# A hybrid encoder layer on one core: sums of weights made by adding transfers in DRAM, and three of eight pairs of k-tiles as seven products

## The chip, the core and the metric

The kernel runs on one core of one Trainium2 chip. Its engines work side by side, each through its own queue in order: TensorE (PE in the profile) multiplies into PSUM, ScalarE (ACT), VectorE (DVE) and GpSimd (POOL) do the elementwise work, SyncE (SP) issues nearly all transfers. Each waits on semaphores of the others. The metric is the device time of one execution in microseconds (us).

## The reference

One layer over 256 tokens of width 2048, all in float32:

```
hn   = rmsnorm(x) ;  proj = hn @ w_in          # 2048 x 18432, nine blocks of 2048 columns
q, v, f_fwd, f_bwd, z_a, b_gate, c_gate, h_b, z_b = split(proj)
o_a  = head_rmsnorm(hgrn2(silu(q), v, f_fwd) + reversed hgrn2(.., f_bwd)) * silu(z_a)   # group A, 16 heads
o_b  = rmsnorm(b_gate * conv3(c_gate * h_b)) * silu(z_b)                                # group B
h    = x + concat(o_a, o_b) @ w_out            # 4096 x 2048
h    = h + (p @ w_ple) * sigmoid(h @ w_ple_gate)
out  = rmsnorm(h)
```

## The kernel before, in words

**Precision.** Every operand of a large product is split into a high part (a cast to fp32r) and a low part (what the cast left). A product is then three matmuls: high by high, high by low, low by high (`three`, L799). ScalarE makes the high part of the weights (L107), VectorE the low one (L108).

**The stream of weights.** `Stream` (L28 to L118) loads weights in order into three raw buffers of a megabyte (`load`, L79, issued by SyncE), and splits them in parts of 1024 columns into five `spl` buffers. `get` (L110) splits three parts ahead of the one that PE is about to use, with priority over other work. A raw buffer is free for the next load when its last part has been split.

**Order of the work.** The kernel is written in the order of PE's matmuls; a scheduler then sets the order on each engine's queue from priorities, and what stands in a queue waits for what is ahead of it. Each k-tile of the large products calls `tick` (L278), which counts and starts work that was put off by `at` (L275). In groups A and B a tick is about 0.7 us of PE.

- Group A: four rounds of two pairs of heads (`two_pairs`, L624). For each pair e = 0, 1 of a round PE makes the two forget gates and q (48 ticks), whose results are moved out of PSUM (`evac`, L378) into `xf` and `qt`; then v and z for both pairs (64 ticks). `mix_forgets` (L428) multiplies `xf` by the tokens' norms on POOL (`by_norms`, L388), and ScalarE takes its sigmoid (L432) and logarithm; `mix_pair` (L485) makes the decays and the products' operands, among them `qc`, `kc` (L529) and `kx` (L535) on POOL. In rounds 2 to 4 the `xf` of pair 1 stands on POOL right behind pair 0's `kx`.
- Group B: eight rounds of four products of 16 ticks (`cg`, `hb`, twice more `hb`), with the convolution on VectorE and POOL.
- The output projection: columns in two steps u of two blocks of 512, each with a half for group A's results (`mixa`) and one for group B's (`mixb`). A half (L805) has 16 k-tiles, taken as eight pairs q. A pair has two k-tiles, two blocks of tokens and two of columns, so eight block products of three matmuls, 24. For q = 3 and 5 (`SUMS`, L171) it is done in seven products, 21 matmuls, from sums of the four weight blocks and of the activations' blocks. The main accumulators take four PSUM banks, the seven-product pairs four more (`extra`); behind the last of these pairs VectorE puts the four extra banks together (L889 to L900: `d`, `v`, `d7`, `v7`), and at the half's end adds the main banks into `hh` (`add_h`, L869).
- The gate, the input embedding and the last norm end the kernel.

**Where the sums are made.** Weights: `sums` (L60) adds blocks on VectorE inside the raw buffer (L66), three additions a pair, between that pair's splits; one raw buffer gives seven blocks in four parts. Activations: `act_sums` (L687) makes and splits `suma` in rounds 4 and 5 of group B and `sumb` at the start of the projection.

Of the kernel before, what the change touches and what calls it, by code (L numbers as in the profile page):

```python
# [17 lines left out]
P = 128  # L18
# [9 lines left out]
class Stream:  # L28
# [19 lines left out]
        self.where += [(j, h) for h in range(k * n // 1024)]  # L48
        return list(range(first, len(self.where)))

    def add_sums(self, *srcs):


        j = len(self.todo)
        self.todo.append((srcs, 2, 1024))
        first = len(self.where)
        self.where += [(j, h) for h in ("singles", "single", "pairs", "more")]
        return list(range(first, len(self.where)))

    def sums(self, j, h):  # L60

        b = self.raws[j].rearrange("p (b n) -> p b n", b=4)

        def add(out, in0, in1):
            with self.tc.high_priority(offset=300):
                self.nc.vector.tensor_tensor(out=out, in0=in0, in1=in1, op=ALU.add)  # L66

        if h == "singles":
            return b[:, 0:2]
        if h == "single":  # L70
            return b[:, 3:4]
        if h == "pairs":
            add(out=b[:, 0:3:2], in0=b[:, 0:3:2], in1=b[:, 2:4])
            return b[:, 0:3:2]
        add(out=b[:, 3], in0=b[:, 0], in1=b[:, 3])
        add(out=b[:, 1], in0=b[:, 3], in1=b[:, 1])
        return b[:, 1:4:2]

    def load(self, j, k0=0, k1=None, pool=None):  # L79
        srcs, k, n = self.todo[j]  # L80
        if j not in self.raws:
            tag = f"raw{j}" if pool else "raw"
            self.raws[j] = (pool or self.rawp).tile([P, 2048], F32, tag=tag, name=f"raw{j}")
        dst = self.raws[j][:, : k * n].rearrange("p (b k n) -> p b k n", b=len(srcs), k=k)
        for b, src in enumerate(srcs):
            self.nc.sync.dma_start(dst[:, b, k0:k1], src[:, k0:k1])

    def open(self, i):
        j, h = self.where[i]
        srcs, k, n = self.todo[j]  # L90
        if j not in self.raws:
            self.load(j)
        part = self.home[i] if i in self.home else self.splp.tile([P, 2048], F32R, tag="spl", name=f"spl{i}")
        if isinstance(h, str):
            r = self.sums(j, h)
            nb = r.shape[1]
            self.parts[i] = part[:, : nb * 1024].rearrange("p (b s n) -> p b s n", b=nb, s=2)
            return r, self.parts[i]
        self.parts[i] = part.rearrange("p (k s n) -> p k s n", s=2, n=n)
        kp, nb = 1024 // n, len(srcs)  # L100
        half = self.raws[j][:, : k * n].rearrange("p (b k n) -> p k b n", b=nb, k=k)[:, kp * h : kp * h + kp]
        if nb == 1:
            return half[:, :, 0, :], self.parts[i]
        return half, part.rearrange("p (k s b n) -> p k s b n", s=2, b=nb, n=n // nb)
# [17 lines left out]
def tile_hymba_encoder(  # L122
# [45 lines left out]
        for c in (B_CG, B_HB, B_BG, B_ZB):  # L168
            blocks[c, i] = sum((ws.add(w_in[c + i, h]) for h in range(2)), [])

    SUMS = (3, 5)  # L171
    oblocks = []
    for u in range(2):
        srcs = [[w_out[2 * u + n, q // 2, :, 2 * (q % 2) : 2 * (q % 2) + 2] for n in range(2)] for q in range(16)]
        oblocks.append([(ws.add_sums if q % 8 in SUMS else ws.add)(*srcs[q]) for q in range(16)])
    gblocks, pblocks = [], []
    for j in range(4):
        if j:
# [96 lines left out]
    def at(dt, fn):  # L275
        pend.append((now[0] + dt, len(pend), fn))

    def tick():  # L278
        now[0] += 1
        due = sorted(e for e in pend if e[0] <= now[0])  # L280
        for e in due:
            pend.remove(e)
        for e in due:
            e[2]()
# [399 lines left out]
    last_two[0]()  # L684


    def act_sums(src, dst, a, s):  # L687


        dve.tensor_tensor(out=a, in0=src[:, :, 0], in1=src[:, :, 1], op=ALU.add)  # L690
        a11, a21, a12, a22 = (a[:, k, m * P : (m + 1) * P] for k in range(2) for m in range(2))
        for o, x, y in ((0, a21, a22), (1, a21, a11), (2, a11, s[:, 0]), (3, a12, s[:, 2])):
            dve.tensor_tensor(out=s[:, o], in0=x, in1=y, op=ALU.subtract)
        act.copy(out=dst[:, :, 0], in_=s)
        dve.tensor_tensor(out=dst[:, :, 1], in0=s, in1=dst[:, :, 0], op=ALU.subtract)


    mixb = None
# [7 lines left out]
    for i in range(8):  # L706
# [31 lines left out]
        if i == 0:  # L738
            assert not pend
            actx.close()  # L740
            bp = mctx.enter_context(tc.tile_pool(name="bp", bufs=1, side="right", reuse_waits="tile"))
            mixb = bp.tile([P, NH, 2, T], F32R, name="mixb")
            og = bp.tile([P, 2, 2, 2, P], F32, name="og")
            suma = bp.tile([P, 2, 4, 2, P], F32R, name="suma")
        if i == 2:
            for e in range(2):
                act.copy(out=og[:, e], in_=kept[e])
        if i in (4, 5):
            a = bp.tile([P, 2, T], F32, tag="sa", name=f"sa{i}")
            b = bp.tile([P, 4, P], F32, tag="sb", name=f"sb{i}")  # L750
            k = 2 * SUMS[i - 4]
            act_sums(mixa[:, k : k + 2], suma[:, i - 4], a, b)
        hi, lo = mixb[:, 2 * i : 2 * i + 2, 0, :], mixb[:, 2 * i : 2 * i + 2, 1, :]
        act.copy(out=hi, in_=cg)
        dve.tensor_tensor(out=lo, in0=cg, in1=hi, op=ALU.subtract)


    def norm_b():
# [21 lines left out]

    sctx = ExitStack()
    spare = sctx.enter_context(tc.tile_pool(name="spare", bufs=1, side="left", reuse_waits="tile"))
    sumb = spare.tile([P, 2, 4, 2, P], F32R, name="sumb")
    tmp = spare.tile([P, 4, 512], F32, name="tmp")

    def gemm_tok(acc, ids, lhs, todo=((0, slice(0, 512)), (1, slice(0, 512)))):

# [17 lines left out]
    def half(main, extra, parts, src, sums):  # L805


        banks = None
        for q, ids in enumerate(parts):
            k = 2 * q  # L810
            if len(ids) == 2:
                for kk in range(2):
                    w = ws.get(ids[kk])[:, 0].rearrange("p s (b n) -> p b s n", b=2)
                    for n in range(2):
                        for m in range(2):
                            ah, al = (src[:, k + kk, s, m * P : (m + 1) * P] for s in range(2))
                            three(main[m][n], al, ah, w[:, n], k + kk == 0, k + kk == NKT - 1)
                        tick()
                continue
            if banks is None:  # L820
                banks = extra()
            z = SUMS.index(q)
            st, sp = z == 0, z == len(SUMS) - 1

            def one(kk, m):
                return [src[:, k + kk, s, m * P : (m + 1) * P] for s in (1, 0)]

            def some(o):
                return [sums[:, z, o, s] for s in (1, 0)]

            w = ws.get(ids[0])
            three(banks[0], *one(0, 0), w[:, 0], st, sp)
            three(main[0][0], *one(1, 0), w[:, 1], False, False)
            tick()
            w = ws.get(ids[1])
            three(main[0][1], *some(3), w[:, 0], False, False)
            w = ws.get(ids[2])
            three(banks[1], *some(0), w[:, 0], st, sp)
            tick()
            three(banks[2], *some(1), w[:, 1], st, sp)  # L840
            w = ws.get(ids[3])
            three(main[1][0], *one(1, 1), w[:, 0], False, False)
            tick()
            three(banks[3], *some(2), w[:, 1], st, sp)
            if sp:
                yield banks

    def h_transposed(u, z):

        for kk in range(2):  # L850
            tag = ("x", "y", "sc0", "sc1")[2 * z + kk]
            tp = psm.tile([P, 512], F32, tag=tag, name=f"ht{u}_{z}_{kk}")
            kt = 8 * u + 4 * z + 2 * kk
            for k in range(2):
# [9 lines left out]
    def four(pool_, name):  # L864
        if pool_ is psg:
            return [psg.tile([P, 512], F32, tag="g", name=f"{name}_{b}") for b in range(4)]
        return [psm.tile([P, 512], F32, tag=t, name=f"{name}_{t}") for t in ("x", "y", "sc0", "sc1")]

    def add_h(m, cs, v, scale):  # L869
        h = hh[:, m, cs]  # L870
# [5 lines left out]
    for u in range(2):  # L876
        cs = [slice(512 * (2 * u + n), 512 * (2 * u + n + 1)) for n in range(2)]
        for src, sums, main, other, scale in ((mixa, suma, psg, psm, False), (mixb, sumb, psm, psg, True)):
            name = f"p{'ab'[scale]}{u}"
            acc = four(main, name)  # L880
            parts = oblocks[u][8 * scale : 8 * scale + 8]
            if u == 0 and not scale:
                for z in range(2):
                    k = 2 * SUMS[z]
                    act_sums(
                        mixb[:, k : k + 2], sumb[:, z], tmp[:, 0:1].rearrange("p b (k t) -> p (b k) t", k=2),
                        tmp[:, 1:2].rearrange("p b (o t) -> p (b o) t", o=4),
                    )
            for q1, q5, q7, q6 in half([acc[0:2], acc[2:4]], lambda: four(other, "e" + name), parts, src, sums):  # L889
                d, v, d7, v7 = (tmp[:, b] for b in range(4))  # L890
                add_h(0, cs[0], q1, scale)
                act.copy(out=d, in_=q1)
                dve.tensor_tensor(out=d, in0=d, in1=q6, op=ALU.subtract)
# [173 lines left out]
```

## Time and profile before

| what | value |
|---|---|
| median of 3 runs | 1122.08 us (1121.8 to 1122.35) |
| the profiled execution, its own time | 1121.94 us |
| its span in the profile | 1120.2 us |
| PE busy | 1110.8 us (99%), granted clock 0.998 |
| VectorE, ScalarE, POOL busy | 788.6, 644.7, 216.5 us |
| group A, group B, projection | to 485, to 839, to about 1011 us |

In a row of the profile's groups stand line, engine, operation, what is written from what, the shapes and the count; then busy time and the mean of one in ns; then the engine's idle time just ahead of it and what ended that. In a timeline a row has the start in us, the duration in us, and in brackets the idle time before it with its releaser. A table by stretches has busy time and count of PE, weight loads, VectorE, ScalarE and POOL, then PE's clock, the share of the 16 DMA engines, and GB/s.

### The profile page before, as it was taken

To read this page: it belongs to the slowest core of one execution; us is meant where nothing else is said; L and a number is where in the kernel's file an instruction comes from. 1 tells how busy PE (TensorE), PEld (TensorE's weight loads), DVE (VectorE), ACT (ScalarE), POOL (GpSimd) and SP (SyncE) were. 2 spreads that over 40 slices of the span, in tenths; PEclk is the share of its full clock that TensorE was granted. 3 is DMA by queue.
4 is the path that set the end of the run, shared out by engine and by line. 5 is a ranking of instruction groups with operands and counts; after the bars stand their busy time and mean duration, and the time that the engine had idled before them with its cause. 6 is when DMAs were issued, how large, how long until landed. Compare 5 with 4: busy or idle time off the path is not lost.

```text
span 1120.2 us, 16504 instructions
## 1 busy us (share of the span) xinstructions
PE 1110.8 (99%) x6506; PEld 955.9 (85%) x6506; DVE 788.6 (70%) x1016; ACT 644.7 (58%) x892; POOL 216.5 (19%) x167
## 2 busy tenths in 40 slices
PE   9999999999999999999999999999999999999997
PEld 8888888888888888888888888888888888888886
DVE  7898476956876587766665566566559988886664
ACT  7796577756765586564454444444545454455553
POOL 1144025300522035211121111111211000000012
PEclk9999999999999999999999999999999999999999
DMA  9756445455545545546555555555556664656552
GB/s 346 281 166 212 154 162 189 156 188 184 196 143 194 183 154 185 189 150 223 174 205 188 188 189 188 188 188 188 189 190 223 225 225 151 225 202 225 202 169 75
DMA packets 41981, 214.27 MB, mean 191 GB/s; under 512 B 4656, under 2 KB 5040, under 8 KB 26288
## 3 DMA queue, kind: packets, MB, share of 16 engines
q1 hardware_dynamic: 41616, 212.88, 55.4%
q8 instruction: 51, 0.84, 0.3%
q10 hardware_dynamic: 288, 0.34, 0.1%
q14 instruction: 26, 0.21, 0.1%
HBM read 211.11 MB, written 2.10 MB: 190 GB/s over the span
## 4 chain that ended last, share of the span: by engine, by line
PE 99%; ACT 0%; DVE 0%; DVEq 0%; issue 0%; ACTq 0%
PE a L351 37%; PE a L349 19%; PE a L372 5%; PE a L370 5%; PE a L371 5%; PE pg L794 3%; PE pg L796 3%; PE pg L795 3%; PE pa L801 2%; PE pa L803 2%; PE pa L802 2%; PE pb_sc L801 1%; PE pb_sc L803 1%; PE pb_sc L802 1%; PE scps L548 1%; PE cx L592 1%
## 5 line engine op out<-in xcount | busy, mean ns | idle before, releaser
L108 DVE TENSOR_TENSOR spl<-raw,spl 128x1024 fp32r<-128x1024 f32 (+2 forms) x414 | 512.7, 1248 | 243.8 <-ACT spl L107 242.6
L351 PE MATMUL a<-xs,spl 128*128 128x512 f32 x1792 | 619.7, 394 | 0.0
L107 ACT CAST spl<-raw 128x1024 fp32r<-128x1024 f32 (+2 forms) x414 | 415.1, 1011 | 307.0 <-PE a L349 162.2
L349 PE MATMUL a<-xs,spl 128*128 128x256 f32 x1792 | 493.6, 278 | 0.0
L351 PEld LDWEIGHTS a<-xs,spl 128*128 128x128 f32 x1792 | 335.0, 188 | 76.1
L349 PEld LDWEIGHTS a<-xs,spl 128*128 128x128 f32 x1792 | 336.2, 188 | 1.5
L370 PE MATMUL a<-spl,xs 128*128 128x512 f32 x256 | 100.8, 394 | 0.0
L372 PE MATMUL a<-spl,xs 128*128 128x512 f32 x256 | 99.8, 390 | 0.0
L371 PE MATMUL a<-spl,xs 128*128 128x512 f32 x256 | 99.7, 389 | 0.0
L383 ACT COPY r<-a 128x256 f32<-128x256 f32 x112 | 40.8, 368 | 54.4 <-PE a L349 54.4
L944 POOL TENSOR_TENSOR hh<-hh,fw 128x512 f32<-128x512 f32 (+1 forms) x9 | 11.3, 1262 | 255.8 <-ACT gt L943 253.2
L372 PEld LDWEIGHTS a<-spl,xs 128*128 128x128 f32 x256 | 48.1, 188 | 10.1
L370 PEld LDWEIGHTS a<-spl,xs 128*128 128x128 f32 x256 | 48.1, 188 | 9.6
L371 PEld LDWEIGHTS a<-spl,xs 128*128 128x128 f32 x256 | 48.1, 188 | 9.5
L794 PE MATMUL pg<-spl,ht 128*128 128x512 f32 (+1 forms) x120 | 45.2, 377 | 0.0
L388 POOL TENSOR_TENSOR xf<-xf,rbc 128x1024 f32<-128x1024 f32 x8 | 19.8, 2479 | 130.9 <-DVE xf L384 124.0
L795 PE MATMUL pg<-spl,ht 128*128 128x512 f32 (+1 forms) x120 | 45.1, 376 | 0.0
L796 PE MATMUL pg<-spl,ht 128*128 128x512 f32 (+1 forms) x120 | 45.1, 375 | 0.0
L529 POOL TENSOR_TENSOR qc<-pf,ge 128x256 f32<-128x256 f32 x16 | 33.8, 2116 | 38.9 <-ACT ge L516 21.0
L801 PE MATMUL pa<-spl,mixa 128*128 128x512 f32 x104 | 40.7, 392 | 0.0
L802 PE MATMUL pa<-spl,mixa 128*128 128x512 f32 x104 | 40.5, 390 | 0.0
L803 PE MATMUL pa<-spl,mixa 128*128 128x512 f32 x104 | 40.5, 390 | 0.0
(263 smaller groups left out, 1270.6 us busy)
## 6 DMA issues: line engine op xcount, KB each, us to landing
raw<-in_w_in_dram SPq DMA_DIRECT2D x106, 1024.0 KB, 4.9
raw<-in_w_in_dram SPq DMA_DIRECT2D x74, 512.0 KB, 4.9
raw<-in_w_out_dram SPq DMA_DIRECT2D x64, 512.0 KB, 4.7
raw<-in_w_gate_dram SPq DMA_DIRECT2D x12, 1024.0 KB, 4.9
raw<-in_w_gate_end_dram SPq DMA_DIRECT2D x8, 512.0 KB, 4.9
xf<-in_xtok_dram SPq DMA_DIRECT2D x2, 1024.0 KB, 11.9
hh<-in_xtok_dram SPq DMA_DIRECT2D x1, 2048.0 KB, 10.1
raw<-in_w_ple_dram SPq DMA_DIRECT2D x4, 512.0 KB, 3.7
```

The lines of the kernel that those rows point to most:

```text
L107: self.nc.scalar.copy(out=v[:, :, 0], in_=r)
L108: self.nc.vector.tensor_tensor(out=v[:, :, 1], in0=r, in1=v[:, :, 0], op=ALU.subtract)
L349: pe.matmul(a[:, :T], lhsT=lhsT, rhs=xs[:, kt, 0, :], start=False, stop=(kt == NKT - 1))
L351: pe.matmul(a, lhsT=lhsT, rhs=xs[:, kt, :, :].rearrange("p s n -> p (s n)"), start=(kt == 0), stop=False)
L370: pe.matmul(acc[m], lhsT=lh, rhs=w[:, kt % 2, 0, :], start=(kt == 0), stop=False)
L371: pe.matmul(acc[m], lhsT=lh, rhs=w[:, kt % 2, 1, :], start=False, stop=False)
L372: pe.matmul(acc[m], lhsT=ll, rhs=w[:, kt % 2, 0, :], start=False, stop=(kt == NKT - 1))
L794: pe.matmul(acc[m], lhsT=lh, rhs=wh, start=(kt == 0), stop=False)
L795: pe.matmul(acc[m], lhsT=lh, rhs=wl, start=False, stop=False)
L796: pe.matmul(acc[m], lhsT=ll, rhs=wh, start=False, stop=(kt == nk - 1))
L801: pe.matmul(acc, lhsT=ah, rhs=w[:, 0], start=start, stop=False)
L802: pe.matmul(acc, lhsT=ah, rhs=w[:, 1], start=False, stop=False)
```

## The change

1. In each half three pairs, q = 2, 3 and 4, are done in seven products, and the pairs are taken in the order 0, 1, 2, 6, 3, 7, 4, 5: one plain pair follows the last seven-product pair, where two did.
2. The sums of weights are no longer made by VectorE. For each of the 12 seven-product pairs there is a tensor `sums` in DRAM. SyncE copies the pair's left and right blocks into it (`prepare`, two transfers of 512 KB), and POOL then issues three transfers that add while they write (`add_up`): 512 KB, then 256 KB, then 256 KB, each on what the one before has written. A table `plan` sets the ticks: preparation n (0 to 11) is copied at tick 150 + 78 n and added at 18, 36 and 54 ticks behind that. Group A ends at tick 640, group B at 1152.
3. In the projection such a pair now fills two raw buffers, one with three single blocks, one with the four sums.
4. Activations: `suma` is made in rounds 1 to 3 of group B (counted from 0), the float32 sums for `sumb` in rounds 2 to 4 (kept in `scm` and `tri`, which group A no longer needs) and split at the projection's start. Two of the four buffers in which the extra banks are put together are now `og`, and the extra banks are taken in another order (`FOUR`).

The core of the diff (line numbers in the profile of before are those of the listing above):

```diff
-    def add_sums(self, *srcs):
+    def add_sums(self, left, right, sums):
         j = len(self.todo)
-        self.todo.append((srcs, 2, 1024))
+        self.todo += [([(left, 0), (right[:, 1:2], 2)], 3, None), ([(sums, 0)], 4, None)]
         first = len(self.where)
-        self.where += [(j, h) for h in ("singles", "single", "pairs", "more")]
+        self.where += [(j, slice(0, 2)), (j, slice(2, 3)), (j + 1, slice(0, 3, 2)), (j + 1, slice(1, 4, 2))]
...
-    SUMS = (3, 5)
+    ORDER, SUMS = (0, 1, 2, 6, 3, 7, 4, 5), (2, 3, 4)
+    dramp = ctx.enter_context(tc.tile_pool(name="dramp", bufs=1, space=bass.MemoryType.DRAM))
...
+    def prepare(n):
+        srcs, sums = prepared[n]
+        for h in range(2):
+            tc.keep_in_program_order(nc.sync.dma_start(sums[:, 2 * h : 2 * h + 2], srcs[h]))
+
+    def add_up(n, step):
+        (_, right), sums = prepared[n]
+        dst, src = ((sums[:, 0:3:2], right), (sums[:, 3], sums[:, 0]), (sums[:, 1], sums[:, 3]))[step]
+        tc.keep_in_program_order(pool.dma_start(dst, src, accum_op=ALU.add))
+
+    plan = {}
+    for n in range(len(prepared)):
+        t = 150 + 78 * n
+        plan[t] = lambda n=n: prepare(n)
+        for step in range(3):
+            plan[t + 18 * (step + 1)] = lambda n=n, step=step: add_up(n, step)
+
     def tick():
         now[0] += 1
+        if now[0] in plan:
+            plan.pop(now[0])()
...
-        if i in (4, 5):
-            a = bp.tile([P, 2, T], F32, tag="sa", name=f"sa{i}")
-            b = bp.tile([P, 4, P], F32, tag="sb", name=f"sb{i}")
-            k = 2 * SUMS[i - 4]
-            act_sums(mixa[:, k : k + 2], suma[:, i - 4], a, b)
...
+        for src, z in ((mixa, i - 1), (mixb, i - SUMS[0])):
+            if 0 <= z < len(SUMS):
+                k = 2 * SUMS[z]
...
-        for q, ids in enumerate(parts):
+        for q, ids in zip(ORDER, parts):
...
-                d, v, d7, v7 = (tmp[:, b] for b in range(4))
+                d, v, d7, v7 = tmps
```

**POOL, in the last round of group A, before.** From pair 0's operands (`qc`, `kc`, `kx`) to pair 1's `xf` and `qt`, the queue has:

```order
L529 TENSOR_TENSOR qc_3763<-pf_3739,ge_3749 128x256
L529 TENSOR_TENSOR kc_3762<-dd_3740,ge_3749 128x256
L535 TENSOR_TENSOR kx_3768<-kc_3762,ge_3749 128x512
L388 TENSOR_TENSOR xf_3770<-xf_3770,rbc 128x1024
L388 TENSOR_TENSOR qt_3771<-qt_3771,rbc 128x512
```

Pair 1's `xf` stands directly behind `kx`.

The same place on POOL, now (`sums_1_4_86` is the tensor of preparation 5):

```order
L546 TENSOR_TENSOR qc_3802<-pf_3778,ge_3788 128x256
L546 TENSOR_TENSOR kc_3801<-dd_3779,ge_3788 128x256
L552 TENSOR_TENSOR kx_3807<-kc_3801,ge_3788 128x512
L284 DMA sums_1_4_86<-in_w_out_dram 256x1x512
L284 DMA sums_1_4_86<-sums_1_4_86 128x512
L405 TENSOR_TENSOR xf_3809<-xf_3809,rbc 128x1024
L405 TENSOR_TENSOR qt_3810<-qt_3810,rbc 128x512
```

Two adding transfers have come between `kx` and `xf`, and the second reads what the first writes. In the two rounds ahead of this one, preparations 1 and 3 put one transfer into the same place; the three of preparations 0, 2, 4 stand together behind the round's last work on POOL, ahead of the next round's first `xf`.

**VectorE, at the end of the projection's first half, before.** The extra banks (`epa`) are put together between splits, and the first main bank (`pa_0`) is added behind that:

```order
L893 TENSOR_TENSOR tmp<-tmp,epa_sc_7724 128x512
L108 TENSOR_TENSOR spl_7880<-raw_7862,spl_7880 128x1024
L894 TENSOR_TENSOR tmp<-epa_y,tmp 128x512
L895 TENSOR_TENSOR tmp<-tmp,epa_sc_7723 128x512
L108 TENSOR_TENSOR spl_7898<-raw_7895,spl_7898 128x1024
L896 TENSOR_TENSOR tmp<-tmp,epa_sc_7723 128x512
L874 TENSOR_TENSOR hh<-pa_0_7606,hh 128x512
```

There the four steps `d`, `v`, `d7`, `v7` are L893 to L896, and `pa_0` comes last.

The same place on VectorE, now:

```order
L920 TENSOR_TENSOR tmp<-tmp,epa_y 128x512
L95 TENSOR_TENSOR spl_7976<-raw_7955,spl_7976 128x1024
L95 TENSOR_TENSOR spl_7994<-raw_7991,spl_7994 128x1024
L921 TENSOR_TENSOR tmp<-epa_sc_7783,tmp 128x512
L905 TENSOR_TENSOR hh<-pa_0_7707,hh 128x512
L95 TENSOR_TENSOR spl_8017<-raw_7991,spl_8017 128x1024
L922 TENSOR_TENSOR og<-tmp,epa_x 128x512
L923 TENSOR_TENSOR og<-tmp,epa_x 128x512
```

The addition of `pa_0` and a split have moved ahead of `d7` and `v7` (L922, L923), which free the last extra bank.

More of the change, by code (lines that the diff above doesn't have):

```diff
@@ L49, in add @@
         return list(range(first, len(self.where)))
-    def add_sums(self, *srcs):
+    def add_sums(self, left, right, sums):
         j = len(self.todo)
-        self.todo.append((srcs, 2, 1024))
+        self.todo += [([(left, 0), (right[:, 1:2], 2)], 3, None), ([(sums, 0)], 4, None)]
         first = len(self.where)
-        self.where += [(j, h) for h in ("singles", "single", "pairs", "more")]
+        self.where += [(j, slice(0, 2)), (j, slice(2, 3)), (j + 1, slice(0, 3, 2)), (j + 1, slice(1, 4, 2))]
         return list(range(first, len(self.where)))
[L60 to L77, printed above, removed]
     def load(self, j, k0=0, k1=None, pool=None):
@@ L83, in load @@
             self.raws[j] = (pool or self.rawp).tile([P, 2048], F32, tag=tag, name=f"raw{j}")
+        if n is None:
+            blocks = self.raws[j].rearrange("p (b n) -> p b n", b=4)
+            for src, b0 in srcs:
+                self.nc.sync.dma_start(blocks[:, b0 : b0 + src.shape[1]], src)
+            return
         dst = self.raws[j][:, : k * n].rearrange("p (b k n) -> p b k n", b=len(srcs), k=k)
@@ L93, in open @@
         part = self.home[i] if i in self.home else self.splp.tile([P, 2048], F32R, tag="spl", name=f"spl{i}")
-        if isinstance(h, str):
-            r = self.sums(j, h)
+        if n is None:
+            r = self.raws[j].rearrange("p (b n) -> p b n", b=4)[:, h]
             nb = r.shape[1]
@@ L169, in tile_hymba_encoder @@
             blocks[c, i] = sum((ws.add(w_in[c + i, h]) for h in range(2)), [])
-    SUMS = (3, 5)
-    oblocks = []
+    ORDER, SUMS = (0, 1, 2, 6, 3, 7, 4, 5), (2, 3, 4)
+    dramp = ctx.enter_context(tc.tile_pool(name="dramp", bufs=1, space=bass.MemoryType.DRAM))
+    oblocks, prepared = [], []
     for u in range(2):
-        srcs = [[w_out[2 * u + n, q // 2, :, 2 * (q % 2) : 2 * (q % 2) + 2] for n in range(2)] for q in range(16)]
-        oblocks.append([(ws.add_sums if q % 8 in SUMS else ws.add)(*srcs[q]) for q in range(16)])
+        for half in range(2):
+            oblocks.append([])
+            for q in ORDER:
+                k = 16 * half + 2 * q
+                srcs = [w_out[2 * u + n, k // 4, :, k % 4 : k % 4 + 2] for n in range(2)]
+                if q in SUMS:
+                    sums = dramp.tile([P, 4, 512], F32, name=f"sums{u}_{half}_{q}")
+                    prepared.append((srcs, sums))
+                    oblocks[-1].append(ws.add_sums(*srcs, sums))
+                else:
+                    oblocks[-1].append(ws.add(*srcs))
     gblocks, pblocks = [], []
@@ L684, in tile_hymba_encoder, with act_sums @@
     last_two[0]()
-    def act_sums(src, dst, a, s):
+    def act_sums(src, a, s):
         dve.tensor_tensor(out=a, in0=src[:, :, 0], in1=src[:, :, 1], op=ALU.add)
@@ L693, in act_sums, with act_split @@
             dve.tensor_tensor(out=s[:, o], in0=x, in1=y, op=ALU.subtract)
+    def act_split(dst, s):
         act.copy(out=dst[:, :, 0], in_=s)
         dve.tensor_tensor(out=dst[:, :, 1], in0=s, in1=dst[:, :, 0], op=ALU.subtract)
+    sumb32 = [*scm, tri]
     mixb = None
@@ L743, in tile_hymba_encoder @@
             og = bp.tile([P, 2, 2, 2, P], F32, name="og")
-            suma = bp.tile([P, 2, 4, 2, P], F32R, name="suma")
+            suma = bp.tile([P, len(SUMS), 4, 2, P], F32R, name="suma")
         if i == 2:
@@ L755, in tile_hymba_encoder @@
         dve.tensor_tensor(out=lo, in0=cg, in1=hi, op=ALU.subtract)
+        for src, z in ((mixa, i - 1), (mixb, i - SUMS[0])):
+            if 0 <= z < len(SUMS):
+                k = 2 * SUMS[z]
+                a = ctmp.tile([P, 2, T], F32, tag="tmp", name=f"sa{i}")
+                if src is mixb:
+                    act_sums(mixb[:, k : k + 2], a, sumb32[z])
+                else:
+                    t = ctmp.tile([P, 4, P], F32, tag="hb", name=f"sb{i}", bufs=2)
+                    act_sums(mixa[:, k : k + 2], a, t)
+                    act_split(suma[:, z], t)
     def norm_b():
@@ L782, in tile_hymba_encoder @@
     spare = sctx.enter_context(tc.tile_pool(name="spare", bufs=1, side="left", reuse_waits="tile"))
-    sumb = spare.tile([P, 2, 4, 2, P], F32R, name="sumb")
-    tmp = spare.tile([P, 4, 512], F32, name="tmp")
+    sumb = spare.tile([P, len(SUMS), 4, 2, P], F32R, name="sumb")
+    tmp = spare.tile([P, 2, 512], F32, name="tmp")
+    tmps = [*(tmp[:, b] for b in range(2)), *(og[:, e].rearrange("p m h t -> p (m h t)") for e in range(2))]
     def gemm_tok(acc, ids, lhs, todo=((0, slice(0, 512)), (1, slice(0, 512)))):
@@ L816, in half @@
                             ah, al = (src[:, k + kk, s, m * P : (m + 1) * P] for s in range(2))
-                            three(main[m][n], al, ah, w[:, n], k + kk == 0, k + kk == NKT - 1)
+                            three(main[m][n], al, ah, w[:, n], q == ORDER[0] and kk == 0, q == ORDER[-1] and kk == 1)
                         tick()
@@ L846, in half @@
                 yield banks
+    FOUR = ("sc0", "sc1", "x", "y")
     def h_transposed(u, z):
         for kk in range(2):
-            tag = ("x", "y", "sc0", "sc1")[2 * z + kk]
+            tag = FOUR[2 * z + kk]
             tp = psm.tile([P, 512], F32, tag=tag, name=f"ht{u}_{z}_{kk}")
@@ L866, in four @@
             return [psg.tile([P, 512], F32, tag="g", name=f"{name}_{b}") for b in range(4)]
-        return [psm.tile([P, 512], F32, tag=t, name=f"{name}_{t}") for t in ("x", "y", "sc0", "sc1")]
+        return [psm.tile([P, 512], F32, tag=t, name=f"{name}_{t}") for t in FOUR]
     def add_h(m, cs, v, scale):
@@ L880, in tile_hymba_encoder @@
             acc = four(main, name)
-            parts = oblocks[u][8 * scale : 8 * scale + 8]
+            parts = oblocks[2 * u + scale]
             if u == 0 and not scale:
[L883 to L888, printed above, removed]
+                for z in range(len(SUMS)):
+                    act_split(sumb[:, z], sumb32[z])
             for q1, q5, q7, q6 in half([acc[0:2], acc[2:4]], lambda: four(other, "e" + name), parts, src, sums):
-                d, v, d7, v7 = (tmp[:, b] for b in range(4))
+                d, v, d7, v7 = tmps
                 add_h(0, cs[0], q1, scale)
```

## The prediction

> **What bounds the kernel now.** I read the chain of waits first, then the busy time by stage, then single instructions of TensorE (PE), ScalarE (ACT), VectorE (DVE) and GpSimd (POOL) where the change puts something new.
>
> ```profile
> span 1120.2 us, 16504 instructions
> PE 1110.8 (99%) x6506; PEld 955.9 (85%) x6506; DVE 788.6 (70%) x1016; ACT 644.7 (58%) x892; POOL 216.5 (19%) x167
> ...
> PE 99%; ACT 0%; DVE 0%; DVEq 0%; issue 0%; ACTq 0%
> ```
>
> ```profile
> 365.00:485.00 120.00, 120.00 (x799) 103.58 (x798) 84.51 (x109) 79.53 (x117) 33.50 (x22) 1.00 0.52 178
> 485.00:839.00 354.00, 354.00 (x2044) 309.64 (x2043) 221.11 (x280) 172.41 (x222) 65.41 (x49) 1.00 0.55 188
> 840.40:884.00 43.60, 43.60 (x194) 36.10 (x194) 39.43 (x57) 25.41 (x32) 3.60 (x2) 1.00 0.67 239
> ```
>
> The chain is PE from end to end. In group A's last pair of heads (365 to 485), in group B (to 839) and in the first half of the output projection (the last row) PE is busy for the whole stretch, at full clock (1.00). No other engine's time is worth anything by itself: fewer matmuls pay at once, and anything that makes PE wait costs at once. Busy matmuls overlap, so the price of one is the distance between starts:
>
> ```profile
> 858.13 0.39 PE L801 MATMUL pa<-spl,suma 128*128 128x512 f32 x1
> ...
> 871.73 0.39 PE L801 MATMUL pa<-spl,mixa 128*128 128x512 f32 x1
> ```
>
> Sixty matmuls lie between these starts: 13.60 / 60 = 0.2267 us each, not the 0.39 in the row.
>
> **The change part by part.** *Third pair as seven products.* Eight products of three matmuls become seven, in one more pair of each of the four halves: 4 x 3 = 12 matmuls, 12 x 0.2267 = 2.7 us, all on the path. Gain 2.7, with no doubt worth pricing.
>
> *Sums of weights leave VectorE.* The 24 additions (20.8 us) go away:
>
> ```profile
> L66 DVE TENSOR_TENSOR raw<-raw 128x512 f32<-128x512 f32 (+1 forms) x24 | 20.8, 867 | 0.5
> L690 DVE TENSOR_TENSOR sa<-mixa 128x512 f32<-128x512 f32 x2 | 2.4, 1188 | 0.0
> ```
>
> VectorE ran beside a PE that never waited, so this gains nothing. The activations' sums that move into group B, six sets with additions of up to 1.19 and four small ones of about 0.29 each, come to some 15 us of VectorE there, where it has 354 - 221 = 133 us free: nothing.
>
> *More to load in the projection.* A half loaded 8 MiB; it now loads 5 + 3 x 1.75 = 10.25 MiB (10.75 MB) in 183 x 0.2267 = 41.5 us, that is 259 GB/s. The row above has 239 GB/s at a DMA share of 0.67, so a full share is some 357 GB/s, and 259 needs 0.73. Three raw buffers still let each load start over 13 us before it is used, by the order of parts and 0.2267 a matmul. Nothing, unless the rate isn't reached (a rival).
>
> *Two banks come free later.* At the end of a half VectorE now has the addition of PE's first finished bank between `v` and `d7`. That bank is finished 9 matmuls (2.0 us) before the half ends; then 0.69 + 1.22 + 0.68 + 0.68 of VectorE (additions and a split) end 1.2 us into the next half, whose eighth matmul (1.6 us in) needs the bank. I take 0.1 at each of three places, 0.3 in all, bounds 0 and 1.
>
> *Copies and accumulating transfers in groups A and B.* The 24 copies are issued by SyncE, wait for nothing, and stand ahead of weight loads that start, by the buffers, five parts of 12 matmuls (5 x 2.7 = 13.6 us) before their first cast; the landings below, 4.9 us for such a load, leave over 8 us for a copied megabyte. Of the 36 accumulating transfers, each waits on POOL for the one before it, with POOL's own work queued behind. Where POOL is idle anyway that costs nothing, and mostly it is:
>
> ```profile
> 389.81 2.40 POOL L388 TENSOR_TENSOR xf<-xf,rbc 128x1024 f32<-128x1024 f32 x1 [40.11 <-DVE xf L384]
> ...
> 489.09 1.30 POOL L456 TENSOR_TENSOR zt<-zt,sz 128x512 f32<-128x512 f32 x1 [19.99 <-ACT sz L455]
> ...
> 542.49 1.30 POOL L388 TENSOR_TENSOR cg<-cg,rbc 128x512 f32<-128x512 f32 x1 [6.42 <-DVE cg L384]
> 553.65 1.29 POOL L713 TENSOR_TENSOR ub<-cg,hb 128x512 f32<-128x512 f32 x1 [9.86 <-DVE hb L384]
> ```
>
> The three transfers in a row of preparations 0, 2 and 4 stand ahead of idle time like the first row's 40 us, those of preparation 6 ahead of 20, and in group B two in a row stand ahead of 6.4 and then 9.9. One place has no cover: preparation 5, in the last pair of group A. Its first transfer is issued when POOL ends `kx`; the second waits for the first to land, and behind it stands `xf`:
>
> ```profile
> 426.68 1.05 POOL L535 TENSOR_TENSOR kx<-kc,ge 128x512 f32<-128x512 f32 x1
> 427.68 2.40 POOL L388 TENSOR_TENSOR xf<-xf,rbc 128x1024 f32<-128x1024 f32 x1
> ```
>
> ```profile
> 424.21 1.28 ACT L432 ACT_TABLE_LOAD   x1
> 430.12 1.06 ACT L432 ACTIVATE xf<-xf 128x1024 f32<-128x1024 f32 x1 [4.62 <-POOL xf L388]
> 431.08 1.03 ACT L107 CAST spl<-raw 128x1024 fp32r<-128x1024 f32 x1
> ```
>
> ```profile
> 432.14 1.23 DVE L108 TENSOR_TENSOR spl<-raw,spl 128x1024 fp32r<-128x1024 f32 x1 [6.60 <-ACT spl L107]
> ...
> 449.70 1.21 DVE L108 TENSOR_TENSOR spl<-raw,spl 128x1024 fp32r<-128x1024 f32 x1
> ...
> 452.64 2.81 DVE L108 TENSOR_TENSOR spl<-raw,spl 128x1024 fp32r<-128x1024 f32 x2 [0.18 <-ACT spl L107]
> ```
>
> ```profile
> 439.44 0.47 PE L370 MATMUL a<-spl,xs 128*128 128x512 f32 x1
> ...
> 455.87 0.39 PE L370 MATMUL a<-spl,xs 128*128 128x512 f32 x1
> ```
>
> `xf` ran with no idle before it, and ScalarE had already waited 4.62 us for it, with the casts of PE's weights queued behind. So a delay d of `xf` moves ScalarE and, behind it, VectorE as a whole: from 432 to 454 VectorE's small gaps are waits for ScalarE and move along. The part of weights that PE starts at 455.87 (six parts of 12 matmuls after 439.44) is ready after the first of the two at 452.64, at about 454.05. Slack 1.8 us: PE waits d - 1.8. Now d: what no row shows is a POOL transfer that accumulates in DRAM. Nearest rows, with the time from issue to landing:
>
> ```profile
> raw<-in_w_in_dram SPq DMA_DIRECT2D x74, 512.0 KB, 4.9
> ...
> xf<-in_xtok_dram SPq DMA_DIRECT2D x2, 1024.0 KB, 11.9
> hh<-in_xtok_dram SPq DMA_DIRECT2D x1, 2048.0 KB, 10.1
> raw<-in_w_ple_dram SPq DMA_DIRECT2D x4, 512.0 KB, 3.7
> ```
>
> ```profile
> 839.28 0.37 SPq L778 DMA_DIRECT2D hh<-in_xtok_dram  x1
> ```
>
> Its result is 512 KB, for which it reads 1024 and writes 512. From 4.9 (512 KB) and 10.1 (2048 KB) a line gives 6.6 for 1024 KB and 8.3 for 1536; I take 7.5. Bounds: 3.7, the fastest 512 KB, and 11.9. POOL's issue of the second I put at 1.0 (SyncE's takes 0.37; bound 2). So d = 8.5, bounds 4.1 and 13.9, and PE waits 6.7, bounds 2.3 and 12.1. A gain is excluded: `xf` can't pass the transfer. The Trainium skill (Collectives: The Full Stack, "The bandwidth ceiling: the fold count and why AG ≠ RS ≠ AR") says that an adding transfer sends two reads through the ring where a copy sends one and runs at half its speed. By that the 4.9 would be 9.8, and the whole 1128.5; no run here shows it yet.
>
> Preparations 1 and 3 put one transfer, without a wait for a landing, ahead of `xf`: an issue of 1.0 is inside the 1.8; at 3 it would cost 1.2 twice.
>
> Sum, against the profiled execution's 1121.94 (span 1120.2 and 1.7 around it): 1121.94 - 2.7 + 0.3 + 6.7 = 1126.2. That execution is 0.14 under the median of the runs, 1122.08, within their spread of 0.55.
>
> **The rivals.** What a measurement of this kernel can tell from no change is about 0.2%, 2.2 us: faster means under 1119.9, slower over 1124.3.
>
> *The wait costs nothing.* If the second transfer doesn't hold POOL until the first has landed, or the casts don't queue behind `xf`, PE loses nothing there: 1121.94 - 2.7 + 0 to 0.3 = 1119.2 to 1119.5, faster. For it: PE never waits now, with four parts split ahead. Against it: ScalarE's 4.62 of waiting for `xf`, and 1.8 us of slack. It decides at d = 1.8 + 0.5. Chance 0.2.
>
> *The wait is short.* With a landing of 3.7 to 4.9 and an issue of 0.4 to 1.0, d is 4.1 to 5.9, PE waits 2.3 to 4.1, and the time is 1121.8 to 1123.6: no change. For it: 4.9 is what loads of that size take at that very place. Against it: twice the reading, and writes to DRAM. The Trainium skill (DMA: Bandwidth & Descriptors, "Anatomy of one DMA — SWDGE (gpsimd) path") gives a transfer issued by POOL 2.0 us and its bytes at 436 GB/s, by which 512 KB land in 3.2 us, an estimate that would give 1121.9; no row here shows such a transfer. Chance 0.25.
>
> *The projection is bound by its loads.* If loads through three buffers hold only the 239 GB/s of the row above, a half takes 10.75 MB / 239 = 45.0 us in place of 41.5, 14 us over four halves: 1133.5 without the wait, slower. It decides from 259 GB/s down. For it:
>
> ```profile
> ACT spl L107 <- DMA raw<-in_w_out_dram: 8.8, 5, 3.0
> ```
>
> ScalarE already waits for landings there, 8.8 us at five places, 3.0 the longest. Against it: PE didn't notice, the share was 0.67, and the row's 239 is what was asked for, not a ceiling. Chance 0.05.
>
> **How the numbers follow.** The forecast, a wait of PE for `xf` that outweighs the matmuls, has the remaining 0.5, with a range of its own from 1124.3 to 1131.6 (a wait of 12.1). With the loads' 0.05 slower has 0.55, same 0.25, faster 0.2. The predicted time is that of the likeliest case, 1126.2. The range runs from the clean case, 1119.2, to 1130.5, which leaves out the longest landings and most of the load-bound case: about 1 in 10, and little below.
>
> **What would show it.** Right: PE without a wait up to about 436, then one or two waits between 439 and 456, several us in all, that end with ScalarE's cast or VectorE's split; ScalarE's wait for `xf` grown from 4.6 to about 13; nothing of the kind in the two earlier pairs; four halves of some 41.5 us in place of 42.2. Wrong: PE as full there as before; a landing of the first accumulating transfer under 4 us; waits of PE in the projection that end with a landing; or waits at `xf` in all three pairs, which would put the price on POOL's issue and not on the landing.

## The result and the profile after

The changed kernel takes 1131.16 us (median of 4 runs, 1129.86 to 1131.79), beside 1122.21 (median of 4 runs, 1121.8 to 1123.38) for the kernel before: a ratio of 1.0077, 95% interval 1.0059 to 1.0094. It is slower by 9 us, where 4 were forecast and the range ended at 1130.5. The profiled execution took 1131.52 with a span of 1129.8.

The page and its chain of waits, to be read against the two lines of before:

```profile
span 1129.8 us, 16629 instructions
...
PE 1111.4 (98%) x6494; PEld 952.7 (84%) x6494; DVE 783.8 (69%) x1012; ACT 652.1 (58%) x902; POOL 250.8 (22%) x203
...
PE 88%; DVE 4%; DMA 4%; ACT 2%; POOL 1%; issue 1%; SPq 0%; DVEq 0%; ACTq 0%; POOLq 0%
```

PE has its 12 matmuls less (6494 against 6506), and a chain that was PE alone now runs through transfers too, and through POOL, ScalarE and VectorE. Four rows on POOL show where that begins (time, duration, and in brackets the idle time before):

```profile
427.69 1.05 POOL L552 TENSOR_TENSOR kx<-kc,ge 128x512 f32<-128x512 f32 x1
428.68 1.05 POOL L284 DMA_DIRECT2D sums<-in_w_out_dram  x1
438.10 0.83 POOL L284 DMA_DIRECT2D sums<-sums  x1 [8.38 <-DMA sums<-in_w_out_dram]
438.65 2.67 POOL L405 TENSOR_TENSOR xf<-xf,rbc 128x1024 f32<-128x1024 f32 x1
```

The second adding transfer of preparation 5 holds POOL for 8.38 us until the first has landed, and `xf` starts 9.97 us after the first was issued. On ScalarE the sigmoid waits for it, with the casts behind:

```profile
425.20 1.28 ACT L449 ACT_TABLE_LOAD   x1
441.35 1.06 ACT L449 ACTIVATE xf<-xf 128x1024 f32<-128x1024 f32 x1 [14.86 <-POOL xf L405]
442.31 1.03 ACT L94 CAST spl<-raw 128x1024 fp32r<-128x1024 f32 x1
```

Before, the same wait of ScalarE was 4.62 us; now it is 14.86. On PE, of all matmuls between 425 and 480 only these had to wait:

```profile
443.39 0.50 PE L387 MATMUL a<-spl,xs 128*128 128x512 f32 x1 [2.71 <-ACT spl L94]
444.65 0.80 PE L388 MATMUL a<-spl,xs 128*128 128x512 f32 x1 [0.76 <-DVE spl L95]
...
462.19 0.50 PE L388 MATMUL a<-spl,xs 128*128 128x512 f32 x1 [2.24 <-DVE spl L95]
```

The four halves of the projection, in the table by stretches (busy time and count of PE, weight loads, VectorE, ScalarE, POOL, then clock, DMA share, GB/s):

```profile
849.50:891.20 41.70, 41.70 (x186) 34.51 (x186) 32.59 (x41) 26.89 (x35) 2.91 (x2) 1.00 0.86 297
891.20:933.00 41.80, 41.75 (x185) 34.24 (x184) 30.12 (x33) 21.97 (x23) 0.00 (x0) 1.00 0.77 259
933.00:977.90 44.90, 43.51 (x200) 35.91 (x199) 36.19 (x41) 24.24 (x27) 0.00 (x0) 1.00 0.70 239
977.90:1019.90 42.00, 41.85 (x185) 34.31 (x185) 31.19 (x34) 21.98 (x23) 0.00 (x0) 1.00 0.76 266
```

In the third above all PE stood idle: 43.51 us busy of 44.90. (It has 1.6 us of transposes in it, as before.) Which engine made PE wait from there on (us in total, times, longest; `og` is the buffer whose writing frees the last extra bank, `ht` are the transposes for the gate):

```profile
PE pa L830 <- DVE og L923: 1.4, 1, 1.4
...
PE ht L887 <- DVE hh L903: 0.6, 1, 0.6
```

Comparing the starts of the same matmuls in both traces (so that a slow restart behind a gap counts too) gives where the 9.6 us between the two spans lie. "Round 4" is the start of the first projection matmul (840.33 before, 849.53 after) less what was lost by the start; "halves" is from there to the first matmul of the gate (1010.88 and 1019.86); "the rest" runs to the end. All are us against the kernel before, from one profiled execution of each version; the median is that of all its runs.

| version | start | round 4 | halves | the rest | median, us |
|---|---|---|---|---|---|
| the change | +1.0 | +8.2 | -0.2 | +0.6 | 1131.16 |
| 1: second transfer later | -0.1 | 0.0 | -0.1 | +0.3 | 1122.08 |
| 2: two more of them early | +1.8 | +23.0 (three rounds) | -0.6 | +2.0 | 1147.67 |
| 3: two plain pairs last | -0.1 | +7.7 | -2.7 | -0.2 | 1126.73 |
| 4: steps first | +0.9 | +7.6 | -2.7 | -0.2 | 1127.54 |
| 5: later, and two plain last | -0.1 | 0.0 | -2.7 | -0.2 | **1119.01** |
| 6: later, and steps first | +0.9 | 0.0 | -2.6 | -0.1 | 1119.79 |
| 7: copies, not additions | 0.0 | +5.2 | +0.2 | +0.6 | 1128.95 |
| 8: sums on VectorE | +1.4 | 0.0 | +1.2 | 0.0 | 1123.37 |

The numbers are those of the experiments below. The start seems to belong to the execution and not to the version: it is within 0.2 of 0 in four and 0.9 to 1.8 us in the others, none of the edits touches it, and the runs of one and the same version lie nearly as far apart (1118.89 to 1120.44 in the fifth). That isn't shown, though: with one profile of each version it can't be told apart from an effect of the version, and both versions with the steps first have 0.9. In the change a cast that came late is the largest piece of it:

```profile
8.77 0.50 PE L368 MATMUL a<-xs,spl 128*128 128x512 f32 x1 [0.96 <-ACT spl L94]
```

### The profile page after: what moved, and what is told of

Its sections match the earlier page's. It is cut to its first block, busy times and chain, and to the rows that moved or that the text cites. A ratio compares the mean times of both kernels' runs of the same rounds, so it can differ in the third digit from the quotient of the medians.

```text
span 1129.8 us, 16629 instructions
## 1 busy us (share of the span) xinstructions
PE 1111.4 (98%) x6494; PEld 952.7 (84%) x6494; DVE 783.8 (69%) x1012; ACT 652.1 (58%) x902; POOL 250.8 (22%) x203
## 4 chain that ended last, share of the span: by engine, by line
PE 88%; DVE 4%; DMA 4%; ACT 2%; POOL 1%; issue 1%; SPq 0%; DVEq 0%; ACTq 0%; POOLq 0%
PE a L368 35%; PE a L366 18%; PE a L388 5%; PE a L389 5%; PE a L387 5%; PE pg L824 2%; PE pg L825 2%; PE pg L823 2%; DVE spl L95 2%; DMA raw<-in_w_out_dram 2%; PE pa L830 1%; PE pa L832 1%; PE pa L831 1%; ACT spl L94 1%; DMA sums<-in_w_out_dram 1%; PE scps L565 1%
## 5 line engine op out<-in xcount | busy, mean ns | idle before, releaser
L95 DVE TENSOR_TENSOR spl<-raw,spl 128x1024 fp32r<-128x1024 f32 (+2 forms) x422 | 518.9, 1241 | 258.1 <-ACT spl L94 256.9
L94 ACT CAST spl<-raw 128x1024 fp32r<-128x1024 f32 (+2 forms) x422 | 421.9, 1008 | 303.0 <-PE a L366 163.2
L284 POOL DMA_DIRECT2D sums<-sums x24 | 19.6, 818 | 82.8 <-DMA sums<-in_w_out_dram 57.6
L830 PE MATMUL pa<-spl,mixa 128*128 128x512 f32 x92 | 36.2, 393 | 1.4 <-DVE og L923 1.4
L832 PE MATMUL pa<-spl,mixa 128*128 128x512 f32 x92 | 35.8, 390 | 0.0
```

The source lines that it names most:

```text
L94: self.nc.scalar.copy(out=v[:, :, 0], in_=r)
L95: self.nc.vector.tensor_tensor(out=v[:, :, 1], in0=r, in1=v[:, :, 0], op=ALU.subtract)
L830: pe.matmul(acc, lhsT=ah, rhs=w[:, 0], start=start, stop=False)
L832: pe.matmul(acc, lhsT=al, rhs=w[:, 0], start=False, stop=stop)
```

## The experiments

**1. The second transfer behind xf.** Preparation 5's second and third transfers come 15 ticks later; one row moves on POOL, nothing else.

```diff
-            plan[t + 18 * (step + 1)] = lambda n=n, step=step: add_up(n, step)
+            plan[t + 18 * (step + 1) + (15 if n == 5 and step else 0)] = lambda n=n, step=step: add_up(n, step)
```

> Preparation 5's second and third transfer come 15 ticks later, so that only its first stands ahead of the last xf on POOL. Theory (POOL waits there for the first landing, and PE loses that delay less 1.8 us): the 8.2 us that PE fell behind in this round go; 1131.2 - 8.2 = 1123.0, within 0.6; PE without a gap from 430 to 480, ScalarE's wait for xf down from 14.9 to about 5.7 (4.6 and one issue of 1.05), no half clock behind it. Rival 1 (the traffic or the issue costs, wherever the transfers stand): still 1129 to 1131. Rival 2 (the wait comes back behind qt, at the next products' scores): PE waits 3 us or more between 455 and 485, 1126 to 1128.

Measured: 1122.08 us, ratio 0.9997 (0.9988 to 1.0006). Nothing is lost in round 4. POOL there, and ScalarE's waits for `xf` (total, times, longest):

```profile
427.54 1.05 POOL L284 DMA_DIRECT2D sums<-in_w_out_dram  x1
428.14 2.86 POOL L405 TENSOR_TENSOR xf<-xf,rbc 128x1024 f32<-128x1024 f32 x1
```

```profile
ACT xf L449 <- POOL xf L405: 18.8, 5, 5.7
```

A transfer that waits for no landing puts `xf` off by 0.6 us, which costs nothing; and behind it the other two cost nothing. Rival 1 (issue or traffic) and rival 2 (another wait) fall. The time came out 0.3 us under the range that I gave; in the profile the start's 1.0 us was absent too.

**2. The same place in two more rounds.** The mirror of it: in preparations 1 and 3 the second transfer moves ahead of `xf`.

```diff
+            plan[t + 18 * (step + 1) - (9 if n in (1, 3) and step == 1 else 0)] = lambda n=n, step=step: add_up(n, step)
```

> The opposite: in preparations 1 and 3 the second transfer comes 9 ticks earlier, so that it stands ahead of xf in rounds 2 and 3 as preparation 5's does in round 4. Theory (place and landing alone decide): 8.2 us each, 1131.2 + 16.4 = 1147.6, within 4; two new waits of ScalarE for xf of about 15 us, two more stretches of PE gaps with a half clock of some 3.4 us. Rival (round 4 is special, its casts run later or its DMA is busier): less than 3 us each, under 1137.

Measured: 1147.67 us, ratio 1.0217 (1.0195 to 1.0239). Rounds 2, 3 and 4 lose 6.4, 8.8 and 7.8. POOL in round 2, and PE behind it in round 3:

```profile
190.69 1.05 POOL L284 DMA_DIRECT2D sums<-in_w_out_dram  x1
198.25 0.84 POOL L284 DMA_DIRECT2D sums<-sums  x1 [6.52 <-DMA sums<-in_w_out_dram]
198.80 2.70 POOL L405 TENSOR_TENSOR xf<-xf,rbc 128x1024 f32<-128x1024 f32 x1
```

```profile
348.24 0.79 PE L388 MATMUL a<-spl,xs 128*128 128x512 f32 x1 [3.49 <-DVE spl L95]
```

Round 4 is not special: place and landing decide. That the median hit 1147.6 so closely is luck: the four runs lie between 1142.73 and 1150.33, the two new losses sum to 15.2, not 16.4, and 1.4 us more was lost behind the halves. A half clock came in only one of the two new places (see the end).

**3. Two plain pairs behind the last seven-product pair.**

```diff
-    ORDER, SUMS = (0, 1, 2, 6, 3, 7, 4, 5), (2, 3, 4)
+    ORDER, SUMS = (0, 1, 2, 5, 3, 4, 6, 7), (2, 3, 4)
```

> Pairs in the order 0, 1, 2, 5, 3, 4, 6, 7: two plain pairs behind the last seven-product pair, all else as in the change. Theory (the projection's missing 2.5 us and the 0.55 at the first transposes come from a tail on VectorE that is one pair too short): no wait of PE for og or hh, the projection's four halves take 2.0 to 2.7 us less, and 1131.2 falls to 1128.0 to 1129.0. Rival (the loads bind, 10.25 MiB a half): no gain, and with two seven-product pairs side by side (3.5 MiB for 9.5 us of PE) PE waits for casts or landings, 1131 to 1134.

Measured: 1126.73 us, ratio 1.0040 (1.0027 to 1.0052). The halves have the full -2.7, and PE waits for neither `og` nor `hh`. VectorE at the end of the second half, first in the change (the third half starts at 932.99), then here (it starts at 931.06):

```profile
930.99 1.22 DVE L95 TENSOR_TENSOR spl<-raw,spl 128x1024 fp32r<-128x1024 f32 x1 [1.75 <-ACT spl L94]
932.13 0.68 DVE L920 TENSOR_TENSOR tmp<-tmp,epb 128x512 f32<-128x512 f32 x1
932.84 0.69 DVE L921 TENSOR_TENSOR tmp<-epb,tmp 128x512 f32<-128x512 f32 x1
933.45 0.74 DVE L903 SCALAR_TENSOR_TENSOR hh<-pb_sc,few,hh 128x512 f32<-128x512 f32 x1
934.11 1.22 DVE L95 TENSOR_TENSOR spl<-raw,spl 128x1024 fp32r<-128x1024 f32 x1
935.24 0.68 DVE L922 TENSOR_TENSOR og<-tmp,epb 128x512 f32<-128x512 f32 x1
935.84 0.68 DVE L923 TENSOR_TENSOR og<-tmp,epb 128x512 f32<-128x512 f32 x1
```

```profile
922.45 0.68 DVE L920 TENSOR_TENSOR tmp<-tmp,epb 128x512 f32<-128x512 f32 x1
...
926.64 0.68 DVE L923 TENSOR_TENSOR og<-tmp,epb 128x512 f32<-128x512 f32 x1
```

In the change the last bank is free 3.5 us into the next half, here 3.7 us before it. And the first row shows what came ahead of it: a split that waited 1.75 us for ScalarE, whose cast had waited 1.92 us for a landing (of a load issued at 922.98, which took 6.8 us, where the median of such loads is 4.8). The last half ends with the same chain, in the second row, ahead of the transposes:

```profile
929.90 2.00 ACT L94 CAST spl<-raw 128x1024 fp32r<-128x1024 f32 x2 [1.92 <-DMA raw<-in_w_out_dram]
...
1015.90 1.05 ACT L94 CAST spl<-raw 128x1024 fp32r<-128x1024 f32 x1 [1.24 <-DMA raw<-in_w_gate_dram]
```

The four steps stood behind a split whose part PE could still do without (experiment 4 puts such splits behind them and PE doesn't notice), and so got the landing's wait as well. Two seven-product pairs side by side did not run out of loads. The gain was larger than I had put it, by the start's 1.0 us, by 0.5 less in round 4 and by the rest's 0.8.

**4. The same end, the steps first.** The order of pairs is the change's; the four steps have priority.

```diff
+                with tc.high_priority(offset=400):
+                    act.copy(out=d, in_=q1)
...
+                    dve.tensor_tensor(out=v7, in0=v, in1=q7, op=ALU.add)
```

> Order of pairs as in the change, but the steps d, v, d7, v7 have priority over splits and over the addition of the main banks, so the last extra bank is free about 1.9 us earlier. Theory (PE waited for that bank): the wait of 1.4 us for og in the third half goes, and with what the other halves lost 1131.2 falls by 1.4 to 2.5, to 1128.7 to 1129.8; the 0.55 at the transposes stays. Rival (VectorE is short there, whichever comes first): PE waits for a split instead, 1131.

Measured: 1127.54 us, ratio 1.0047 (1.0035 to 1.0060). Again the full -2.7, with another order on one engine and nothing else: the loss was VectorE's order, not its load; a landing from DRAM could reach PE only through that order. At the end of the second half the last step is now this, 1.4 us before the third half starts (931.92) and so 4.9 us earlier than in the change, where I had put 1.9:

```profile
929.87 0.68 DVE L924 TENSOR_TENSOR og<-tmp,epb 128x512 f32<-128x512 f32 x1
```

The wait at the transposes went too, which I had not expected; it was the same lateness, one step on.

**5 and 6. Both cures.** Experiment 1's line with experiment 3's (5), and with experiment 4's (6).

> Both changes of the first two gains together: preparation 5's later transfers 15 ticks later, and the pairs in the order 0, 1, 2, 5, 3, 4, 6, 7. Theory (the two losses are independent, 8.2 in group A and 2.5 to 3.3 in the projection, and behind them stand the 2.7 us of 12 matmuls): 1122.1 - 2.7 = 1119.4, 1119.0 to 1120.0, a ratio to the kernel before of 0.9970 to 0.9985. Rival (one hides the other, or the order costs at the landings): 1121 to 1123.

> Preparation 5's later transfers 15 ticks later, and the steps d, v, d7, v7 first, in the order of pairs of the change. Theory: as the version with two plain pairs last, 1119.0 to 1120.0. Rival (VectorE has no reserve with one plain pair left): 1120.5 to 1122.

Measured: 1119.01 us, ratio 0.9974 (0.9963 to 0.9984), and 1119.79, ratio 0.9976 (0.9967 to 0.9985). Both beat the kernel before, by about a quarter of a per cent. Of the fifth, the chain and the four halves:

```profile
PE 99%; DMA 0%; ACT 0%; DVE 0%; DVEq 0%; issue 0%; ACTq 0%
```

```profile
840.20:881.80 41.60, 41.60 (x185) 34.47 (x185) 34.41 (x45) 26.75 (x35) 2.91 (x2) 1.00 0.87 308
881.80:923.30 41.50, 41.50 (x184) 34.35 (x183) 31.69 (x35) 21.81 (x23) 0.00 (x0) 1.00 0.77 258
923.30:966.60 43.30, 43.30 (x201) 36.02 (x200) 34.50 (x40) 23.99 (x27) 0.00 (x0) 1.00 0.75 251
966.60:1008.10 41.50, 41.50 (x185) 34.37 (x184) 30.27 (x33) 21.72 (x23) 0.00 (x0) 1.00 0.74 250
```

PE is busy throughout at 308 GB/s in the first half: the loads don't bind.

**7. What the adding costs.** The 36 transfers on POOL copy.

```diff
-        tc.keep_in_program_order(pool.dma_start(dst, src, accum_op=ALU.add))
+        tc.keep_in_program_order(pool.dma_start(dst, src))
```

> The change with the 36 transfers on POOL copying instead of adding, so the sums of weights in the output are left out; order and sizes the same. Theory 1 (the time is that of a transfer from DRAM to DRAM, as SyncE's copies of 512 KB show with 7.5 us): the first landing stays at 7 to 8.5, PE falls back by 6 to 8, 1129 to 1131. Theory 2 (adding doubles what the transfer sends, half the speed): the landing falls to 4 to 5, PE falls back by 3 to 4.5, 1126 to 1127.5.

Measured: 1128.95 us (four runs, 1127.15 to 1130.42), ratio 1.0060 (1.0044 to 1.0075), between the two theories. The issues (count, size, median us to landing), first with adding, then with copying:

```profile
sums<-in_w_out_dram SPq DMA_DIRECT2D x24, 512.0 KB, 7.5
...
sums<-in_w_out_dram POOLq DMA_DIRECT2D x12, 512.0 KB, 8.2
sums<-sums POOLq DMA_DIRECT2D x24, 256.0 KB, 5.6
```

```profile
sums<-in_w_out_dram POOLq DMA_DIRECT2D x12, 512.0 KB, 5.0
sums<-sums POOLq DMA_DIRECT2D x24, 256.0 KB, 4.8
```

```profile
427.64 0.67 POOL L284 DMA_DIRECT2D sums<-in_w_out_dram  x1
434.37 0.53 POOL L284 DMA_DIRECT2D sums<-sums  x1 [6.06 <-DMA sums<-in_w_out_dram]
434.90 2.42 POOL L405 TENSOR_TENSOR xf<-xf,rbc 128x1024 f32<-128x1024 f32 x1
```

My own theory 1 falls: from SyncE's 7.5 for such a copy POOL's can't be told, which lands in 5.0. (SyncE issues two of them 0.6 us apart; whether that or the issuing engine makes the difference, no run shows.) Adding takes 3.2 us more. The Trainium skill (Collectives: The Full Stack, "The bandwidth ceiling: the fold count and why AG ≠ RS ≠ AR") tells of collectives between cores that the step that adds runs at half the speed of the one that copies, because it needs two source reads. For these transfers on one core that doesn't hold as it stands: the adding one took 1.6 times as long at 512 KB and 1.2 times at 256. At this place, where weight loads run beside it, the copy held POOL for 6.7 us, the adding one for 9.4, so PE still lost 5.2.

**8. No sums in DRAM.** Three seven-product pairs in experiment 3's order, with the sums from VectorE inside the raw buffer as before.

```diff
-        self.todo += [([(left, 0), (right[:, 1:2], 2)], 3, None), ([(sums, 0)], 4, None)]
...
-        self.where += [(j, slice(0, 2)), (j, slice(2, 3)), (j + 1, slice(0, 3, 2)), (j + 1, slice(1, 4, 2))]
+        self.todo.append((srcs, 2, 1024))
...
+        self.where += [(j, h) for h in ("singles", "single", "pairs", "more")]
```

> No sums in DRAM: the three seven-product pairs (order 0, 1, 2, 5, 3, 4, 6, 7) have their sums of weights from VectorE inside the raw buffer, as the kernel before had for two. Theory 1 (VectorE, 39.4 of 43.6 us busy in a half before, has no room for three more additions, 2.6 us, in 41.6): PE waits for splits in every half, 1 to 3 us each, 1122 to 1129. Theory 2 (VectorE's work of the main banks and splits shifts enough): as the version in DRAM without its wait, 1119.0 to 1120.0, and the transfers were not needed.

Measured: 1123.37 us, ratio 1.0009 (1.0000 to 1.0018). The halves take 3.9 us more than in experiment 5 and eat up the 2.7. Comparing starts as above, 1.9 of it lie in the first half and 1.4 in the third, 0.3 in each of the others, and not 1 to 3 in every half as theory 1 had it. PE's waits for VectorE, and VectorE in the first half:

```profile
PE ht L897 <- DVE hh L913: 1.0, 1, 1.0
PE epa_sc L841 <- DVE spl L108: 0.7, 1, 0.7
...
PE epa_x L840 <- DVE mixa L507: 0.4, 1, 0.4
```

```profile
840.00:882.00 42.00, 40.88 (x185) 33.08 (x185) 37.59 (x50) 25.27 (x34) 3.82 (x2) 1.00 0.60 210
```

VectorE is busy 37.6 of 42 us here and 34.4 in experiment 5. So the transfers pay for the third pair: well placed, they are worth some 4 us, from 1123.37 to 1119.01.

## Why the prediction was right or wrong, point by point

The direction and the place were right, the sum too small, and most of what it lacked was the ends of halves: 1126.2 + 1.5 (the wait) + 3.0 (the ends of halves, 3.3 in place of 0.3) + 1.0 (the start) = 1131.7, within 0.2 of the profiled 1131.52.

- **Gain, 2.7 us:** right. Experiments 3 to 6 have -2.6 to -2.7 in the halves.
- **One place without cover, preparation 5:** right, shown by experiments 1 and 2. Preparations 1 and 3 (one transfer ahead of `xf`), 0, 2, 4 and 6, group B and the copies cost nothing: PE has no other wait until the projection.
- **PE waits d - 1.8:** right. In the change `xf` moved by 9.98 us against the PE of before (its start's 1.0 taken off), and PE lost 8.2; in experiments 3 and 4 it was 9.5 and 7.7, and 9.4 and 7.6. With the copies it was 7.2 and 5.2. Round 3 of experiment 2 lost 2.4 more than that (see the end). In the change the long second wait, at 462.19, came one part of weights earlier than I had it; the part that I had named added the last 0.2.
- **Landing 7.5 and issue 1.0, d = 8.5:** mis-sized by 1.5. The second transfer was issued 9.4 us after the first, and `xf` started 0.55 behind that. A landing of 8.2 is the median of the 12; they spread from 7.2 to 10.5, and this one, 8.9, stood beside weight loads. The Trainium skill's 2.0 us and bytes at 436 GB/s (DMA: Bandwidth & Descriptors, "Anatomy of one DMA — SWDGE (gpsimd) path"), 3.2 by estimate, would have been short even for the copy's 5.0.
- **Banks free later, 0.3 us, bounds 0 and 1:** this is the step that failed. It cost 2.5 in the halves and 0.8 behind them. I had started the sum when the first main bank is finished, 2.0 us before the half ends, and taken it that VectorE has `d` and `v` behind it by then and is free. At the end of the second half `d` itself (L920) started only 0.9 us before the end: it stood in the queue behind a split, which waited for a cast, which waited for a landing. The first half, without that wait, freed the bank 1.7 us into the next, where I had put 1.2. Against the same matmuls of experiment 6, with the same order of pairs and the steps first, the second, third and fourth halves lost 0.3, 1.7 and 0.4 us at that bank, where I had 0.1 each. The 0.8 at the transposes behind the last half had no term at all.
- **Loads bind the projection:** wrong as a rival, shown by experiment 5; but a landing that ScalarE waited for did reach PE, by way of VectorE's queue.
- **The wait is short, or nothing:** fell with the landing of 8.9.
- **The range:** the forecast's own range, 1124.3 to 1131.6, held the result, but by luck: its upper end came from a wait of 12.1 us for `xf`, not from the ends of halves. I had cut the range at 1130.5, treating those ends as if they could give no more than 1.

## What to carry to other kernels

A transfer that waits for another one's landing is an instruction that blocks its whole queue: count what stands behind it on that engine, and move it behind that work, not merely later in the program. When buffers or banks are freed by a chain of small steps, price the chain from the first instruction ahead of it in the queue that can itself wait, not from the moment its input is ready. Here two changed lines of placing were worth 12 us, the idea itself 3.

## What the runs showed of the hardware

- A 512 KB transfer from DRAM to DRAM issued by POOL lands in 5.0 us when it copies and 8.2 when it adds (medians of 12), 256 KB in 4.8 and 5.6 (of 24). POOL's issue took 0.67 and 1.05 us at 512 KB.
- PE's granted clock (the third number from the end of the row) fell to half behind the waits. In the change:

```profile
444.30:447.70 3.40, 3.05 (x7) 2.47 (x8) 2.19 (x5) 3.39 (x7) 0.00 (x0) 0.50 0.02 5
```

It lasted 3.4 us. It lay between the two waits, of which the second ends with VectorE, and seems to have cost nothing of its own in the end: round 2 of experiment 2, without a half clock, lost 6.4 for a delay of 8.1, the same d - 1.8. In experiment 2's round 3 it began in the second wait and lasted 6.8 us, and that round lost 8.8 us for a delay of 8.2, where by d - 1.8 it would be 6.4:

```profile
349.00:354.00 5.00, 5.00 (x14) 3.90 (x13) 4.79 (x6) 4.97 (x8) 1.22 (x2) 0.52 0.65 220
```

The Trainium skill (TensorE: Matmul & The Clock Gate, "Part 1: The HAM clock gate") has a window of 3.4 us after which an idle PE is throttled, free-running, so that the same gap may or may not be caught. That fits in part: the half clocks lasted 3.4 and 6.8 us, one such window and two, and the same waits of 0.9, 0.8 and 3.5 us in rounds 2 and 3 of experiment 2 brought it only in round 3. But in the change it came after waits of 2.7 and 0.8 us, neither as long as the window. No run here was made to test it.
